# Earlier loads and a new order of small steps in a hybrid attention kernel: mask and two weights loaded a stage sooner, first output blocks split inside the last gates, new tokens' steps that end a slot, a later turn of mixer B's factors

## The chip, the core and the metric

The program runs on one core of one Trainium2 chip. A core has five engines that each work through a queue of their own, in order: TensorE (PE; its weight loads are shown apart as PEld) multiplies matrices, VectorE (DVE), ScalarE (ACT) and GpSimd (POOL) work on elements, and SyncE (SP) only issues transfers here. Sixteen DMA engines move data. The metric is the device time of one execution in microseconds (us), lower is better, given as the median of several runs.

## The reference, cut to what matters

One layer of a decoder: a prompt of 2048 tokens and 8 new tokens, width 1024.

```python
def _prompt_layer(x, w_in, sinks, w_o, ln_g, ln_b):
    qa, ka, va, ga, qb, kb, vb, gb = _project(x, pos, w_in)      # rotary on the first quarter of each head
    parts = []
    for _, d in ((128, 1), (512, 4), (2048, 16)):                # mixer A: 8 heads, three strided bands
        m, den, o = _band_partial(_dilate(qa[:, :, :, None], d), _dilate(ka, d), _dilate(va, d))
        parts.append((_undilate(m, b, s, d), _undilate(den, b, s, d), _undilate(o, b, s, d)))
    oa = _merge(parts)
    m, den, o = _band_partial(qbg, kb, vb)                       # mixer B: 8 heads, band of 128, sinks
    ob = _merge([(m, den, o)], sink)
    mix = concat([oa * silu(ga), ob * silu(gb)])
    return layer_norm(ALPHA * x + mix @ w_o)
```

`_merge` weighs partial outputs by exp(m - max) and divides by the summed denominators; the factor of each row and pattern is what the text calls **the factors**. The new tokens do the same against a cache. All results are float32; the large products are made from a high and a low part (h and l) of each operand, three matmuls for one.

## The kernel before, in words

**Stages.** First (0 to about 242 us) the projections of K and Q. Then the values' stage (242 to 378 us): V for all tokens in two column groups, and between its matmuls the new tokens' attention of mixer A, whose cached values (`vc`, six loads of 1 MB) feed the `soa` matmuls of line 444. Then the attention stage (378 to about 980 us), then the output projection with the layer norm.

**The attention stage** is written out by hand inside `tc.manual_schedule` (line 1117): each engine gets the instructions of this region in the order in which the program emits them. Instructions outside the region are ordered by a planner on a simulated clock; it may put them between the region's instructions but cannot change the order of those. The main loop runs over 66 **groups** i. A group makes the scores of one quarter of a job (a job is one pair of heads at one dilation: 12 for mixer A, 4 for mixer B), turns (transposes) the weights of group i-1 and multiplies the values of group i-2. It has four **slots** (sl = 0 to 3). In each slot `advance(870 ns)` draws matmuls from `follow`, which is a stream of other PE work: first the projections of mixer B's queries and of the gates in three passes (line 628, 24 matmuls for one block, each worth n / 2.4 ns), then the first blocks of the output projection (line 671, each worth 213 ns). A `yield None` in `follow` ends the slot's share. Then `step()` runs `tick()` (pending small jobs; one or two quarters of a raw weight are split on GpSimd) and moves the first of the **chains** on by one step.

**Chains** wait their turn: only the first of the list moves. `merge_b` (line 945), one for each of mixer B's four pairs, computes the factors on DVE and ACT (952 to 960), turns them on PE (line 965), writes them to memory (970), fetches them spread over 64 partitions on GpSimd's queue (982) and multiplies the outputs (992), the last pair's on DVE alone. A step between two `yield`s takes one slot. Its turn waits for slot 3 (`while where[0] < 3`).

**Raw weights.** `Parts` (line 113) puts four quarters of a weight in a queue; `raw_step` loads two quarters in a tick into one of four small buffers and splits a quarter on GpSimd three ticks later. The weights of QB2 and G0, third and fourth of the first pass, come in this way from the stage's first tick on; those of QB0 and QB1 are split before.

**The mask** `mk` (128 x 768) is loaded after the values' stage (line 563) and negated (line 1121) ahead of the first `weights` (line 832), whose `mk` operand is its 128 columns from 128 on in the first job.

**PSUM.** Gate blocks (`pg`), the new tokens' small products of mixer B (`scb`, `spt`, `sob`, `spo`, made by `sample("b")` one step after each gate block of the last pass) and the first output blocks share two banks (tag `mm`). A gate block frees its bank when ACT (line 167) and, one tick later, DVE (line 171) have read it.

**The first output blocks.** At the start of the last gate block row `gated(0)` loads gate and mixed output of tokens 0 to 255. `out_weights` (line 720) asks for the last two output weights (four empty slots), splits that block (739, 740), and then runs 12 matmuls for each half of token blocks 0 and 1, loads and splits the next 256 tokens after that, with three more empty slots, and goes on with token blocks 2 and 3. What the loop hasn't drawn when it ends is emitted outside the region (lines 1162 to 1164).

Of the kernel before, what the change touches and what calls it, by code (L numbers as in the profile page):

```python
# [11 lines left out]
F32 = mybir.dt.float32  # L12
# [38 lines left out]
def hymba_step(ctx, tc, xt, xs, xr, wq, wv, wo, tab, msk, ident, diag, sinks, lng, lnb,  # L51
# [61 lines left out]
    class Parts:  # L113


        def __init__(self, src, hl=None):
            self.hl, self.left = hl, 4
            raws.extend([self, src, k0, None, 0] for k0 in range(0, 8, 2))
# [9 lines left out]
    def raw_step(now=False):  # L128

        for r in raws:  # L130
            r[4] += r[3] is not None
        for _ in range(2):
            if raws and raws[0][0].hl and raws[0][3] is not None and (now or raws[0][4] >= 3):
                p, _, k0, w, _ = raws.popleft()
                h, l = p.hl
                G.tensor_copy(h[:, k0:k0 + 2], w)
                G.tensor_sub(l[:, k0:k0 + 2], w, h[:, k0:k0 + 2].bitcast(F32))
                p.left -= 1
        for r in [r for r in islice(raws, RAW) if r[3] is None][:2]:
            r[3] = at.tile([128, 2, 128], F32, name="raw", bufs=RAW)  # L140
            dma(r[3], r[1][:, r[2]:r[2] + 2])
# [197 lines left out]

    def sample(nm, sp, sk):  # L340
# [29 lines left out]
        if A:  # L370
            z = z.rearrange("p n i c -> p n (i c)")
        else:
            snc = sp.tile([128, 1], F32, name="snc")
            dma(snc, dram(sinks, 0, [[0, 16], [1, 8], [1, 1]]))
            kcs = []
            for t in range(2):
                kc = sk.tile([128, 4, w], F32, name="kc", tag="cache", bufs=2)
                dma(kc[:, :, :w - 1], kcb[:, 4 * t:4 * t + 4])
                kcs.append(kc)
            yield  # L380
            yield
            for t, kc in enumerate(kcs):
                V.tensor_copy(kc[:, :, w - 1], kself[:, 0, 4 * t:4 * t + 4])
            yield
        p = ps.tile([128, 512], F32, name="sc" + nm, tag="mm")
# [29 lines left out]
        yield  # L415
        pt = ps.tile([128, 512], F32, name="spt", tag="mm")
# [16 lines left out]
        for t in range(2):  # L433
            if A or t == 0:
                oa = ps.tile([128, 512], F32, name="so" + nm, tag="mm")
# [33 lines left out]
        yield  # L469
        pt = ps.tile([128, 512], F32, name="spo", tag="mm")  # L470
# [7 lines left out]
    first = {}  # L478

    def load_first():  # L480

        for n, src, h0 in (("k", ks, 2), ("q", qa, 0)):
            t = first[n] = kp.tile([128, SEQ], F32, name=n)
            for h in range(2):
                dma(t[64 * h:64 * h + 64], src[:, h0 + h, :SEQ])
        v = first["v"] = kp.tile([128, 16, 128], F32, name="v")
        dma(v, vs[1].rearrange("(p r) c -> p r c", r=16))
# [77 lines left out]
    def stream(passes):  # L565

        with tc.tile_pool(name="gw", bufs=1, side="right", reuse_waits="tile") as gw, \
# [31 lines left out]
            for i in (2, 3):  # L599
                ws[passes[0][i]] = Parts(wq[TILES.index(passes[0][i])])  # L600
                weights(i, passes[0][i])
            for pi, names in enumerate(passes):
# [7 lines left out]
                for c, c2 in zip(route, route[1:] + [None]):  # L610
# [3 lines left out]
                    if c2 is None:  # L614
                        for name in more:
                            ws[name] = Parts(wq[TILES.index(name)])
                        if not more:
                            head.append(gated(0))
                            wo_parts.update((i, Parts(wo[:, i].rearrange("p (a b) -> p a b", b=128))) for i in (4, 5))
                    for i, name in enumerate(names):  # L620
# [12 lines left out]
                        if news:  # L633
                            next(news, None)
                        if c2 is None:
                            if not more and i < 2:
                                soon(lambda i=i: first_wo(i), 1)
                            for e in range(i, len(more) if name == names[-1] else min(i + 1, len(more))):
                                soon(lambda e=e, name=more[e]: weights(e, name), 1)
# [4 lines left out]
    queries, wo_parts = [], {}  # L644
# [59 lines left out]
    head = []  # L704
# [15 lines left out]
    def out_weights():  # L720
# [6 lines left out]
        nxt = head[0]  # L727
        first.clear()
        for j in range(2):
            t, g = nxt  # L730
# [4 lines left out]
            for _ in range(1 if j == 0 else 2):  # L735
                yield None
            h, l = [oh.tile([128, 4, 256], F32R, name="h" + a) if j else kept.tile([128, 4, 256], F32R, name="h" + a, tag="p%d" % (i + 2))
                    for i, a in enumerate("hl")]
            V.tensor_mul(t, t, g)
            split(h, l, t, V)  # L740
            yield None
            if j == 0:
                nxt = gated(1)
            for tb, x in zip((2 * j, 2 * j + 1), xs_):
# [6 lines left out]
                first[tb] = x, 4  # L751

# [3 lines left out]
    class Job:  # L756
# [69 lines left out]
        def weights(self, g, us):  # L826
            for u in us:
# [4 lines left out]
                V.tensor_tensor_reduce(sm[:, :w], self.s[:, h, n % 4, :w], mk[:, MI[self.d], 256 - w:], -0.125, 3.0e38,  # L832
# [112 lines left out]
    def merge_b(job):  # L945
# [16 lines left out]
        while where[0] < 3:  # L962
            yield
# [153 lines left out]
    with tc.manual_schedule(engines=set(ENGINES)):  # L1117
# [3 lines left out]
        V.tensor_scalar(mk, mk, -1.0, None, op0=OP.mult)  # L1121
        jobs[0].fetch_q(0)
        for i in range(N + 2):
# [19 lines left out]
            for sl in range(4):  # L1143
# [6 lines left out]
                where[0] = sl  # L1150
                advance(RATE / 4 if i else RATE / 2)
# [10 lines left out]
    ascope.close()  # L1162
    for _ in follow:
        pass
# [176 lines left out]
```

## Time and profile before

| | |
|---|---|
| median of 3 runs | 1188.15 us (1187.61 to 1189.95) |
| profiled execution, its own time | 1187.53 us |
| its span, first to last instruction | 1185.7 us |
| mean granted TensorE clock | 0.987 |
| PE, PEld, DVE, ACT, POOL busy | 95, 85, 46, 37, 35 % of the span |
| DMA | 230.14 MB, mean 194 GB/s |

A span lies inside the time of its execution, 1.8 us shorter here. Matmul ends are modelled, so PE busy does not mean PE at its peak. Idle time of an engine counts only where the end hangs on it. Three things are read together: the waits of PE (who let it go on, and after how long), the granted clock in short stretches, and the timeline of the other engines at the same moment. In a timeline row stand start, duration, engine, line, operation, output<-inputs, count, and in brackets the idle time before it and what ended it.

### The profile page before, as it was taken

The numbers are of one execution on the slowest core, as the hardware profiler recorded it, in microseconds if no ns is written. First come the engines' busy times: TensorE is split into PE (matmuls) and PEld (weight loads), VectorE is DVE, ScalarE is ACT, GpSimd is POOL, SyncE is SP. The second block draws the span as 40 slices with busy tenths as digits, with TensorE's granted clock in tenths as the row PEclk, the third lists the DMA queues.
The fourth block names the chain that finished last, engine by engine and source line by source line (L and its number), as shares of the span: only waits on it lengthen the run. The fifth ranks groups of instructions, "written<-read, shape, count | busy, mean of one in ns | idle before, by whom it ended". The sixth has DMA issues, their size and how long they took to land.

```text
span 1185.7 us, 23404 instructions
## 1 busy us (share of the span) xinstructions
PE 1131.9 (95%) x8614; PEld 1002.3 (85%) x8614; DVE 547.6 (46%) x1784; ACT 437.9 (37%) x1416; POOL 416.2 (35%) x559
## 2 busy tenths in 40 slices
PE   7999999999999899999999999999998988999995
PEld 7899999997978788898888789888887866688884
DVE  6532000101002465465566556666657664775543
ACT  4300011111101566556656555555554541232221
POOL 2243010310001300046715603670574454476541
PEclk9999999999999999999999999999999998999998
DMA  8854988366396664489688868968989667556521
GB/s 277 257 146 144 272 272 280 108 195 203 124 325 200 188 163 141 136 193 202 172 235 185 197 211 193 195 159 239 229 184 276 183 189 231 169 153 199 186 87 69
DMA packets 194002, 230.14 MB, mean 194 GB/s; under 512 B 34608, under 2 KB 160208, under 8 KB 193504
## 3 DMA queue, kind: packets, MB, share of 16 engines
q1 hardware_dynamic: 188640, 211.87, 59.3%
q0 software_dynamic: 5248, 16.78, 9.2%
q8 instruction: 67, 1.10, 0.4%
q14 instruction: 47, 0.39, 0.1%
HBM read 158.52 MB, written 70.07 MB: 193 GB/s over the span
## 4 chain that ended last, share of the span: by engine, by line
PE 69%; DMA 13%; POOL 4%; DVE 4%; ACT 3%; issue 3%; SPq 1%; DVEq 0%; POOLq 0%; ACTq 0%
PE po L671 14%; PE pg L628 13%; PE pv L526 7%; PE ps_s L824 7%; PE ps_o L875 6%; DMA F<-fd 6%; PE ps_pt L854 5%; PE ps L151 4%; PE pmm L151 4%; PE ppt L151 4%; PE po L151 3%; ACT pe L835 2%; DMA wvf<-in_wv 1%; POOL F L1054 1%; POOL oT L1055 1%
## 5 line engine op out<-in xcount | busy, mean ns | idle before, releaser
L835 ACT ACTIVATE pe<-sm,st 128x256 f32<-128x256 f32 (+1 forms) x512 | 236.6, 464 | 206.2 <-DVE st L832 204.8
L832 DVE CUSTOM_DVE_ANT_0 sm<-ps_s,mk 128x256 f32<-128x256 f32 (+1 forms) x512 | 180.2, 375 | 182.8 <-PE ps_s L824 116.2
L628 PE MATMUL pg<-gx,gw 128*128 128x256 f32 (+1 forms) x1104 | 166.7, 294 | 4.4 <-DVE mixS L476 2.1
L628 PEld LDWEIGHTS pg<-gx,gw 128*128 128x128 f32 x1104 | 142.5, 192 | 5.1 <-issue 4.3
L854 PE MATMUL ps_pt<-idt,pe 128*128 128x128 f32 x848 | 135.2, 280 | 5.7 <-ACT oT L892 2.8
L860 DVE COPY pT<-ps_pt 128x512 f32<-128x512 f32 x176 | 120.6, 685 | 6.8 <-PE ps_pt L854 6.6
L1040 POOL DMA_DIRECT2D F<-fd x64 | 41.2, 647 | 209.7 <-DMA fd<-wts 202.9
L854 PEld LDWEIGHTS ps_pt<-idt,pe 128*128 128x128 f32 x848 | 96.4, 142 | 19.6 <-issue 8.7
L875 PE MATMUL ps_o<-pT,v 128*64 128x128 f32 (+1 forms) x1120 | 106.8, 335 | 0.0
L875 PEld LDWEIGHTS ps_o<-pT,v 128*64 128x64 f32 x1120 | 70.1, 137 | 39.5 <-issue 16.5
L835 ACT ACTIVATION_READ_ACCUMULATOR pe<-sm,st 128x1 f32 x512 | 96.3, 188 | 0.0
L824 PE MATMUL ps_s<-k,qo 64*128 64x256 f32 (+1 forms) x768 | 91.8, 379 | 0.0
L628 PE MATMUL pg<-gx,gw2h 128*128 128x256 f32 (+1 forms) x368 | 75.6, 294 | 2.1 <-ACT spe L405 2.1
L824 PEld LDWEIGHTS ps_s<-k,qo 64*128 64x128 f32 x768 | 66.7, 188 | 12.4 <-issue 1.3
L526 PE MATMUL pv<-wvh,xh 128*128 128x384 f32 (+1 forms) x224 | 69.6, 311 | 0.0
L526 PE MATMUL pv<-wvh,xl 128*128 128x384 f32 (+1 forms) x224 | 69.5, 310 | 0.0
L526 PE MATMUL pv<-wvl,xh 128*128 128x384 f32 (+1 forms) x224 | 69.4, 310 | 0.0
L628 PEld LDWEIGHTS pg<-gx,gw2h 128*128 128x128 f32 x368 | 58.7, 192 | 2.4 <-ACT spe L405 2.4
L671 PE MATMUL po<-wl,mho 128*128 128x512 f32 x192 | 59.7, 392 | 0.0
L538 ACT ACTIVATE vf<-pv 128x384 f32<-128x384 f32 (+1 forms) x32 | 14.0, 437 | 111.8 <-PE pv L526 61.6
L628 PE MATMUL pg<-gx,gw2l 128*128 128x256 f32 (+1 forms) x184 | 54.2, 294 | 0.0
L259 POOL TENSOR_TENSOR wl<-w,wh 128x512 fp32r<-128x512 f32 x18 | 24.2, 1356 | 82.8 <-DVE wh L258 82.8
(260 smaller groups left out, 2521.0 us busy)
## 6 DMA issues: line engine op xcount, KB each, us to landing
gx<-xd SPq DMA_DIRECT2D x80, 512.0 KB
F<-fd POOLq DMA_DIRECT2D x80, 192.0 KB, 7.1
gs<-th SPq DMA_DIRECT2D x64, 128.0 KB
v<-vs SPq DMA_DIRECT2D x28, 256.0 KB
xd<-xh SPq DMA_DIRECT2D x12, 512.0 KB
xd<-xl SPq DMA_DIRECT2D x12, 512.0 KB
kc<-in_kca SPq DMA_DIRECT2D x8, 768.0 KB
vc<-in_vca SPq DMA_DIRECT2D x6, 1024.0 KB
```

The source lines that it names most:

```text
L151: T.matmul(p[:, :n], a[:, kt, :], b, start=k == 0, stop=k == 23)
L259: (V if between else G).tensor_sub(l[:, k0:k0 + 4], w, h[:, k0:k0 + 4].bitcast(F32))
L526: T.matmul(p[:, :w], l, r[:, kt, :w], start=k == 0, stop=k == 23)
L628: T.matmul(p[:, :n], a[:, kt, :], b[:, kt % 2, :n], start=kt + e == 0, stop=kt == 7 and e == 2)
L671: T.matmul(p, a, b[:, nh * 4:nh * 4 + 4].rearrange("p a b -> p (a b)"), start=first and k == 0, stop=last and k == end)
L824: T.matmul(s[:, h, n % 4, :w], self.Q[g][r, n % 4 * 128:n % 4 * 128 + 128], self.keys(n)[r], start=True, stop=True)
L832: V.tensor_tensor_reduce(sm[:, :w], self.s[:, h, n % 4, :w], mk[:, MI[self.d], 256 - w:], -0.125, 3.0e38, op0=OP.add, op1=OP.min, accum_out=m)
L835: S.activation(p[:, :w], sm[:, :w], AF.Exp, scale=-1.0, bias=m, accum_out=den)
L854: T.transpose(pt[:, h, j], self.P[h, n][:, a:a + 128], idt)
L860: V.tensor_copy(t, pt)
L875: T.matmul(o[64 * h:64 * h + 64, a:a + 128 * len(ns)], v[:, cv, kv:kv + 64], t[:, h, j:j + len(ns)].rearrange("p a b -> p (a b)"), start=n ...
L1040: G.dma_start(F[a * 64:a * 64 + 64], dram(fd, a * 3 * SEQ + c * 256, [[0, 64], [SEQ, 3], [1, 256]]))
```

## The change

Four edits. **Loads:** `load_first`, in the values' stage, also loads the first job's 128 mask columns (64 KB) and the raw weights of QB2 and G0 (two loads of 512 KB), ahead of the first K, Q and V; they take a buffer of the K and of the Q tiles. The quarters of these two weights are then split in the first four ticks with no load of their own. The whole mask is negated three slots into group 1. **First output blocks:** `first_split`, seven ticks after the last gate block row begins, splits tokens 0 to 255; the next 256 are split right after token block 0's products; four of the empty slots are gone, and what is left of `follow` is emitted inside the region. **New tokens:** after each of their four steps that makes a product in PSUM, `follow` yields 1200 ns, which ends the slot and takes from the next. **Factors:** for the first three of mixer B's pairs two more `yield`s stand ahead of the turn.

```diff
-        def __init__(self, src, hl=None):
+        def __init__(self, src, hl=None, here=None):
             self.hl, self.left = hl, 4
-            raws.extend([self, src, k0, None, 0] for k0 in range(0, 8, 2))
+            raws.extend([self, src, k0, None if here is None else here[:, k0:k0 + 2], 3] for k0 in range(0, 8, 2))
...
         for r in raws:
-            r[4] += r[3] is not None
+            r[4] = r[4] + 1 if r[3] is not None else 0
...
     def load_first():
+        early_w = kp.tile([128, 2, 8, 128], F32, name="raw01", tag="k", bufs=2)
+        early_m = kp.tile([128, 128], F32, name="mk1", tag="q", bufs=2)
+        dma(early_m, msk[:, 0, 128:256])
+        for i in range(2):
+            dma(early_w[:, i], wq[TILES.index(FIRST[2 + i])])
+        first["m"], first["w"] = early_m, early_w
...
-                ws[passes[0][i]] = Parts(wq[TILES.index(passes[0][i])])
+                ws[passes[0][i]] = Parts(wq[TILES.index(passes[0][i])], None, first["w"][:, i - 2])
...
                         if not more:
                             head.append(gated(0))
+                            early_split.append(soon(first_split, 7))
...
                         if news:
+                            parting.clear()
                             next(news, None)
+                            if parting:
+                                yield 1200
...
+    def first_split():
+        t, g = head.pop()
+        h, l = [kept.tile([128, 4, 256], F32R, name="h" + a, tag="p%d" % (i + 2)) for i, a in enumerate("hl")]
+        V.tensor_mul(t, t, g)
+        split(h, l, t, V)
+        halves.append((h, l))
+        head.append(gated(1))
...
+        here = blocks(0)
+        yield None
+        for j in range(2):
+            h, l = halves[j]
+            for tb, x in zip((2 * j, 2 * j + 1), here):
...
                 first[tb] = x, 4
+                if tb == 0:
+                    here = blocks(1)
+                    t, g = head.pop()
+                    h2, l2 = [oh.tile([128, 4, 256], F32R, name="h" + a) for a in "hl"]
+                    V.tensor_mul(t, t, g)
+                    split(h2, l2, t, V)
+                    halves.append((h2, l2))
...
-                V.tensor_tensor_reduce(sm[:, :w], self.s[:, h, n % 4, :w], mk[:, MI[self.d], 256 - w:], -0.125, 3.0e38,
+                V.tensor_tensor_reduce(sm[:, :w], self.s[:, h, n % 4, :w], (mk[:, MI[self.d], 256 - w:] if self is not jobs[0] else first["m"]), -0.125, 3.0e38,
...
         while where[0] < 3:
             yield
+        if job.of.pair < 3:
+            yield
+            yield
         pst = ps.tile([128, 512], F32, name="pst", tag="pt", bufs=2)
...
-        V.tensor_scalar(mk, mk, -1.0, None, op0=OP.mult)
+        V.tensor_scalar(first["m"], first["m"], -1.0, None, op0=OP.mult)
...
+                if i == 1 and sl == 3:
+                    V.tensor_scalar(mk, mk, -1.0, None, op0=OP.mult)
...
-    ascope.close()
-    for _ in follow:
-        pass
+        ascope.close()
+        for _ in follow:
+            pass
```

`parting` gets an entry in `sample` ahead of each of the four PSUM tiles; `blocks(j)` loads the two input blocks that `for tb, x` uses, as the removed lines did.

More of the change, by code (lines that the diff above doesn't have):

```diff
@@ L338, in hymba_step @@
                     EMIT[TILES[i][0]](pw, NC, p, TILES[i], c0, n)
+    parting = []
     def sample(nm, sp, sk):
@@ L384, in sample @@
             yield
+        parting.append(0)
         p = ps.tile([128, 512], F32, name="sc" + nm, tag="mm")
@@ L415, in sample @@
         yield
+        parting.append(1)
         pt = ps.tile([128, 512], F32, name="spt", tag="mm")
@@ L434, in sample @@
             if A or t == 0:
+                parting.append(2)
                 oa = ps.tile([128, 512], F32, name="so" + nm, tag="mm")
@@ L469, in sample @@
         yield
+        parting.append(3)
         pt = ps.tile([128, 512], F32, name="spo", tag="mm")
@@ L642, in stream @@
                 pass
-    queries, wo_parts = [], {}
+    queries, wo_parts, early_split = [], {}, []
     ready, merged, resident = [], [], []
@@ L702, in norm @@
         dma(y[tb * 128:tb * 128 + R], x[:R])
-    head = []
+    head, halves = [], []
+    def first_split():
[5 more added lines that the diff above has]
+        head.append(gated(1))
     def gated(j):
@@ L726, in out_weights, with blocks @@
         oh = wscope.enter_context(tc.tile_pool(name="oh", bufs=1, side="right", reuse_waits="tile"))
-        nxt = head[0]
         first.clear()
-        for j in range(2):
-            t, g = nxt
+        if not halves:
+            early_split[0].run()
+        def blocks(j):
             xs_ = [(oh if tb < 3 else kp).tile([128, D], F32, name="xh%d" % tb, **(dict(tag="k", bufs=2) if tb == 3 else {}))
@@ L734, in out_weights @@
                 dma(x, xr[tb * 128:tb * 128 + 128])
[L735 to L744, printed above, removed]
+            return xs_
+        here = blocks(0)
[3 more added lines that the diff above has]
+            for tb, x in zip((2 * j, 2 * j + 1), here):
                 cols = slice(tb % 2 * 128, tb % 2 * 128 + 128)
```

## The prediction

> **What bounds the kernel now.** First the page: PE is the bound in total, so the question is where it waits and where its clock falls. Columns: busy us, share of the span, instructions.
>
> ```profile
> span 1185.7 us, 23404 instructions
> PE 1131.9 (95%) x8614; PEld 1002.3 (85%) x8614; DVE 547.6 (46%) x1784; ACT 437.9 (37%) x1416; POOL 416.2 (35%) x559
> ```
>
> Second the waits of PE between 300 and 1020 us: who let it go on, us in total, times, longest.
>
> ```profile
> PE pg L628 <- ACT qf L181: 4.7, 1, 4.7
> PE pst L965 <- DVE wts L960: 4.7, 2, 2.4
> PE po L671 <- DVE xh L750: 3.4, 1, 3.4
> ...
> PE po L671 <- ACT hh L108: 2.6, 2, 2.3
> PE pg L628 <- ACT spe L405: 2.1, 1, 2.1
> PE pg L628 <- DVE mixS L476: 2.1, 1, 2.1
> PE pg L628 <- issue: 1.7, 1, 1.7
> PE po L671 <- DVE hl L109: 1.0, 2, 0.5
> ```
>
> Each edit answers one of these: the loads the first, the factors the second, the output blocks the third, fourth and last, the new tokens the three between. Third, short stretches. Columns: us, busy us (instructions) of PE, PEld, DVE, ACT, POOL, granted clock, DMA share, GB/s.
>
> ```profile
> 390.20:393.60 3.40, 3.40 (x18) 3.18 (x17) 0.00 (x0) 0.00 (x0) 2.12 (x5) 0.51 0.65 200
> 840.70:844.10 3.40, 1.28 (x22) 0.87 (x22) 2.33 (x8) 3.22 (x14) 2.95 (x5) 0.99 0.92 221
> 844.10:847.50 3.40, 3.40 (x16) 3.40 (x17) 2.82 (x8) 0.73 (x3) 3.31 (x6) 0.50 0.88 169
> 878.30:881.70 3.40, 3.40 (x18) 3.40 (x18) 2.53 (x5) 0.60 (x2) 2.95 (x6) 0.51 0.41 42
> 960.20:963.60 3.40, 3.40 (x18) 1.93 (x16) 1.53 (x8) 1.09 (x4) 0.00 (x0) 0.51 0.39 102
> 980.70:984.10 3.40, 3.40 (x9) 2.67 (x10) 2.24 (x7) 0.26 (x1) 1.88 (x4) 0.51 0.99 275
> 1001.20:1004.60 3.40, 3.40 (x10) 2.67 (x9) 0.81 (x2) 0.00 (x0) 1.50 (x3) 0.52 0.90 236
> 927.90:931.30 3.40, 3.40 (x35) 2.52 (x36) 1.81 (x10) 0.88 (x4) 0.00 (x0) 1.00 1.01 319
> ```
>
> A stall is often followed by 3.4 us at half clock (0.50 to 0.52), which loses 1.7 us more: six such stretches stand here. The starts lie on one grid of some 3.4 us (960.2, 980.7 and 1001.2 are 20.5 apart, six steps). Not every stall pays: behind the one of 2.3 us that ends at 927.73 the clock stayed at 1.00 (last row).
>
> [...]
>
> **The change, part by part.** The sum is against the profiled execution, 1187.5 us (span 1185.7 and 1.8 around it); the median of the runs shown is 0.6 higher.
>
> *Loads.* Timeline (start, duration, engine, line, operation, output<-inputs, count, [idle before <-releaser]) and two longer stretches:
>
> ```profile
> 379.14 6.09 PE L628 MATMUL pg<-x,gw 128*128 128x264 f32 x48
> 385.22 0.56 DVE L1121 TENSOR_SCALAR mk<-mk 128x768 f32<-128x768 f32 x1 [8.32 <-DMA mk<-in_msk]
> 385.70 0.40 POOL L136 CAST gw2h<-raw 128x256 fp32r<-128x256 f32 x1 [14.06 <-DMA raw<-in_wq]
> 389.93 0.64 PE L628 MATMUL pg<-x,gw2h 128*128 128x264 f32 x2 [4.70 <-ACT qf L181]
> 323.50:358.00 34.50, 31.90 (x268) 27.55 (x266) 2.26 (x4) 2.69 (x7) 1.43 (x2) 1.00 1.05 332
> 358.00:378.00 20.00, 19.53 (x180) 17.61 (x176) 6.03 (x18) 3.45 (x9) 4.47 (x6) 1.00 0.50 146
> ```
>
> The mask lands at 385.2, after 8.3 us in which DVE has nothing to do, the raw weight not before 385.7; the DVE and ACT work of group 0 queues behind the negation, and the `pg` bank that PE wants comes free only behind that, at 389.9. With both resident the first negation runs at once, POOL splits four ticks early, and eight raw loads leave SP's queue there. The second negation (0.56 us, three slots into group 1) lies under PE's gate matmuls; uncovered it would cost 0.56. So -4.7, and -1.7 for the half-clock stretch at 390.2. The price: 64 KB and two times 512 KB, 1.11 MB, join the values' stage. At 332 GB/s, where the engines were full (share 1.05), they take 3.4 us; the 20 us after that have a share of 0.50. I take a third, 1.1, since most queue positions fall where there is slack; bounds 0 and 5.1 (all of it on PE, and one half-clock stretch). Net -5.3, bounds -6.4 to -1.3.
>
> *New tokens.* Their small steps wait for ACT or DVE work that the same slot queued before. Turns and gates in a slot:
>
> ```profile
> 856.41 0.60 PE L854 MATMUL ps_pt<-idt,pe 128*128 128x128 f32 x4
> 856.76 1.19 PE L628 MATMUL pg<-gx,gw 128*128 128x256 f32 x8
> ...
> L860 DVE COPY pT<-ps_pt 128x512 f32<-128x512 f32 x176 | 120.6, 685 | 6.8 <-PE ps_pt L854 6.6
> ```
>
> A slot that ends there lets PE go on with the job's turns; two fill 0.35 to 0.4 us each (856.41 to 856.76), so each of the three waits (2.1, 1.7, 2.1) shrinks by 0.8: -2.4. I count one half-clock stretch as avoided, -1.7. Against that, four slots lose their gate matmuls, and the copies of their turns (0.69 us) are covered only by the next turns (0.35): four slots, two copies, 0.34 each, +2.7. The put-off work itself, 4 x 1200 / 106.7 = 45 matmuls (5.7 us at 6.09 / 48), is not lost but ends the gates five to six slots later. Net -1.4; bounds -9.3 (5.9 of waits and two stretches gone) and +2.7 (only the copies).
>
> *Factors.* Rows of pair 1's turn and what follows:
>
> ```profile
> 927.73 0.27 PE L965 MATMUL pst<-idt,wts 128*32 128x128 f32 x1 [2.29 <-DVE wts L960]
> 932.33 2.09 POOL L982 DMA_DIRECT2D F<-fd  x4 [4.80 <-DMA fd<-stT]
> 937.06 1.81 POOL L992 TENSOR_TENSOR oT<-oT,F 128x768 f32<-128x768 f32 x1 [2.64 <-DMA F<-fd]
> ```
>
> Two steps are two slots, far above the 2.3 us by which `wts` is late. So -4.7, and -1.7 for the stretch at 960.2. The turn now falls in slot 1 instead of 3, between the job's turns, with the same two banks: a copy of 0.69 may delay each of three: 0 to +2.1, I take +1.0. Net -5.4, bounds -6.4 to -4.3. The price is elsewhere: only the first of the chains moves, so each pair passes two slots (and what it waits for slot 3) to the next. Counting the `yield`s, turns of pairs 0 to 2 go from slot 3 of groups 56, 59, 62 to slot 1 of 57, 61, 65, and pair 3's from group 65 to nine steps behind the loop.
>
> *The tail.* From the last value matmuls to the new tokens' block. DVE rows, the group of multiplications, its landing times, and the chain that ended last:
>
> ```profile
> 975.06 1.95 PE L875 MATMUL ps_o<-pT,v 128*64 128x256 f32 x20
> 980.38 0.38 DVE L952 SCALAR_TENSOR_TENSOR mn<-snk,st 128x32 f32<-128x32 f32 x1
> 983.21 0.19 DVE L960 SCALAR_TENSOR_TENSOR wts<-wts,dn 128x32 f32<-128x32 f32 x1
> 984.70 0.69 DVE L750 SCALAR_TENSOR_TENSOR xh<-xh,po 128x512 f32<-128x512 f32 x1 [1.29 <-PE po L671]
> 990.97 1.22 DVE L739 TENSOR_TENSOR ht<-ht,hg 128x1024 f32<-128x1024 f32 x1
> 993.31 1.23 DVE L109 TENSOR_TENSOR hl<-ht,hh 128x1024 fp32r<-128x1024 f32 x1 [1.13 <-ACT hh L108]
> L992 DVE TENSOR_TENSOR oT<-oT,F x6: 692/952/1059, 914.1 to 1006.0; 128x768 f32<-128x768 f32 x5, 128x512 f32<-128x512 f32 x1
> DMA to landing us min/median/max: 2.8/4.3/10.0
> 1010.81 7.00 PE po L161 x64
> 1017.81 146.93 PE po L671 x634
> ```
>
> Before: 977.0 to 1010.8, 33.8 us, with 96 first-block matmuls (22.3 us at 146.93 / 634 = 0.232), two half-clock stretches and the waits. After, block 0 is split inside the gates, so PE starts at once; but DVE keeps the written order, in which pair 2's multiplication stands ahead of the sum of the first block (L750), of the split of block 1 and of pair 3's factors. From pair 2's turn, near the end of the values: to `F`'s issue 4.6 (927.73 to 932.33), landing 4.7 (to 937.06), POOL's part 1.8, DVE's 0.95, L750 0.7, split 3.6 (990.97 to 994.54), factors 3.0 (980.38 to 983.40): 19.4 to pair 3's turn. PE has a third of the 96 matmuls ahead of it (32 or 33, 7.7 us) and stands for about 11.7. From that turn 4.6 + 4.7 + 0.95 + 1.0 (a second issue) + 4.7 + two multiplications of 0.7, and 2.8 for the last output block (12 matmuls), 20.1; queued behind each are L750s, hence `po`'s two banks. Together 39.5, and two half-clock stretches as now, 3.4: 42.9. The planner may put part of the 7.0 us of the new tokens' block (L161, outside the region) into the gap; I take 2.5 (bounds 0 and 7.0): 40.4, which is +6.6 (bounds +2.1 and +9.1, above that the first rival). The splits on POOL of the last two weights come some steps later, under the same gap.
>
> Sum: -5.3 - 1.4 - 5.4 + 6.6 = -5.5, so **1182.0 us**.
>
> **The rivals.**
>
> *The chain in the tail sets the end* (slower). Nothing is pulled into the gap (+2.5) and one `F` of pair 3 lands after 10.0 us, the longest row above, instead of 4.3 (+5.7): 1182.0 + 8.2 = 1190.2. It decides when the tail exceeds 33.8 + 12.1 (the three gains) = 45.9. For it: two of these loads stand in a row, and DMA shares of 0.90 to 0.99 in the stretches there. Against: the median of 4.3.
>
> *PE stays fed.* The tail has more than I see that doesn't hang on DVE, and the waits of today (3.4 + 2.6 + 1.0 = 7.0) and two half-clock stretches (3.4) go: -12.1 - 10.4 = 1165.0. For it: block 0's products start under the last values. Against: the DVE order.
>
> *The early loads only move the wait, and the tail is no worse or better.* -6.4 + 3.4 + 1.7 = -1.3; the edits in the gates give nothing, because a slot that ends meets the next unready chain: about 1186.0, within what can be told. For it: share 1.05 in the values' stage.
>
> **How the numbers follow.** Forecast 0.40 (own range 1177.5 to 1186, from the whole block pulled in, 4.5 below, to loads and new tokens half way to their upper bounds, 4.0 above), slower rival 0.25, fed PE 0.10, no change 0.25. A measurement of this kernel can tell some 0.2%, 2.4 us (the runs shown span 1187.61 to 1189.95). Of the last, 0.03 falls below that bound and 0.02 above; of the slower rival 0.03 falls within it. Faster 0.40 + 0.10 + 0.03 = 0.53, same 0.20 + 0.03 = 0.23, slower 0.22 + 0.02 = 0.24. The range reaches 10 down towards the fed PE, of which it leaves out most, and up to 1194, where a second landing is late by two thirds of 5.7: 1172 to 1194 leaves out about 0.07 below and 0.10 above.
>
> **What would show it.** Loads: PE's wait at 385 gone and POOL's `gw2h` cast before 380 us; right if values still end near 378.05, wrong if later by 2 or more. New tokens: waits of `pg` between 840 and 912 about 3.5 instead of 6. Factors: no wait of `pst` within the gates. Tail: a new wait `pst` <- `wts` of 8 to 12 us behind the last values, then `po` <- `xh`; the L161 block before or after the last `po`; three of the six half-clock stretches gone (390, 960 and one of 844 and 878). Wrong: a tail under 30 us (the fed PE), or over 46 (slower).

## The result and the profile after

The changed kernel takes 1197.66 us (median of 5 runs, 1196.86 to 1205.08) against 1187.61 (5 runs) for the kernel before: ratio 1.0097, 95% interval 1.0068 to 1.0127, some 11.5 us slower (the medians differ by 10.1). The forecast was 1182.0 and faster. The profiled execution took 1199.82 us.

First the page of the changed kernel, and four long pieces of the chain that ended last (start, us, what). Line numbers are those of the changed kernel: 628 became 642, 671 became 688, 750 became 774, 860 became 891, 965 became 999, 982 became 1016, 992 became 1026.

```profile
span 1197.8 us, 23412 instructions
PE 1133.0 (95%) x8614; PEld 1002.5 (84%) x8614; DVE 544.6 (45%) x1785; ACT 438.2 (37%) x1416; POOL 416.2 (35%) x559
```

```profile
986.26 8.99 DMA F<-fd
1008.39 4.75 DMA mgo<-gs
1022.86 7.00 PE po L161 x64
1029.86 146.94 PE po L688 x634
```

PE does the same work (8614 matmuls, 1133.0 us against 1131.9) in a span 12.1 us longer. The new tokens' block (L161) starts 12.05 us later, at 1022.86 against 1010.81, and from there on both kernels are alike. So all is lost before it. The first two pieces, a load of pair 2's factors and one of gates for a later output block, come up again below. Now the waits of PE between 300 and 1040 us (us in total, times, longest):

```profile
PE po L688 <- DVE xh L774: 10.4, 3, 7.4
PE ps_pt L885 <- DVE pT L891: 8.3, 11, 2.5
PE pst L999 <- DVE wts L991: 6.8, 1, 6.8
...
PE spo L477 <- DVE od L473: 2.8, 1, 2.8
PE pg L642 <- ACT th L424: 1.7, 1, 1.7
PE pg L642 <- DVE mixS L482: 1.5, 1, 1.5
...
PE ps_s L855 <- ACT vf L551: 1.2, 1, 1.2
PE pg L642 <- ACT spe L408: 0.8, 1, 0.8
```

The copies' waits in the kernel before, for comparison:

```profile
PE ps_pt L854 <- DVE pT L860: 2.4, 6, 1.1
```

The waits that the edits were aimed at are gone or smaller: `qf` 4.7 (gone), `pst` within the gates 4.7 (gone), the new tokens' 2.1, 1.7 and 2.1 (now 1.7, 1.5 and 0.8). But others stand in their place: 2.8 and 1.2 at the end of the values' stage, copies (`pT`) 8.3 instead of 2.4, and behind the loop 10.4 + 6.8 instead of 3.4 + 2.6 + 1.0.

By stage, from the timeline of PE (us; "tail" is from the end of the last value matmuls to the new tokens' block):

| | before | changed | changed, second profile |
|---|---|---|---|
| first scores (the values' stage ends) | 378.05 | 384.27 | 381.07 |
| first scores of group 2 | 393.57 | 394.85 | 392.31 |
| last values end | 977.0 | 977.1 | 973.4 |
| tail | 33.7 | 45.7 | 44.9 |

Of the three gains of 12.1 us that the forecast had ahead of the tail nothing is left at the end of the values in the first profile and 3.6 us in the second, and the tail is 11 to 12 us longer. The chain of the tail, in a timeline of the changed kernel (start, us, engine, line, operation, [idle before <-releaser]):

```profile
978.57 0.27 PE L999 MATMUL pst<-idt,wts 128*32 128x128 f32 x1
978.69 1.84 SPq L141 DMA_DIRECT2D raw<-in_wo  x4
983.62 1.48 SPq L141 DMA_DIRECT2D raw<-in_wo  x2
985.15 0.90 SPq L761 DMA_DIRECT2D xh<-in_xr  x2
984.68 2.10 POOL L1016 DMA_DIRECT2D F<-fd  x4
991.11 0.69 DVE L774 SCALAR_TENSOR_TENSOR xh<-xh,po 128x512 f32<-128x512 f32 x1 [11.32 <-DMA xh<-in_xr]
991.86 1.22 PE L688 MATMUL po<-wl,hh 128*128 128x512 f32 x2 [7.44 <-DVE xh L774]
995.37 0.96 DVE L1026 TENSOR_TENSOR oT<-oT,F 128x768 f32<-128x768 f32 x1 [3.57 <-DMA F<-fd]
996.85 1.62 DVE L780 TENSOR_TENSOR ht<-ht,hg 128x1024 f32<-128x1024 f32 x1
999.59 1.22 DVE L109 TENSOR_TENSOR hl<-ht,hh 128x1024 fp32r<-128x1024 f32 x1 [1.12 <-ACT hh L108]
1002.49 0.19 DVE L991 SCALAR_TENSOR_TENSOR wts<-wts,dn 128x32 f32<-128x32 f32 x1
1002.83 0.37 PE L999 MATMUL pst<-idt,wts 128*32 128x128 f32 x1 [6.77 <-DVE wts L991]
```

PE starts block 0 at once (978.6), and stops after two halves: the sums wait for `xh`, whose loads stand behind six raw loads in SyncE's queue. Then VectorE waits for pair 2's `F` (995.37), issued on GpSimd at 984.68, and behind that multiplication stand the second sum, the second split and pair 3's factors. PE has nothing for 7.4 and 6.8 us. The granted clock adds to it (columns as before: us, busy of the engines, clock, DMA share, GB/s):

```profile
920.90:924.30 3.40, 2.84 (x14) 2.62 (x14) 2.66 (x8) 1.46 (x4) 3.18 (x6) 0.50 0.17 47
934.50:937.90 3.40, 3.40 (x16) 3.09 (x18) 1.50 (x5) 1.58 (x4) 0.00 (x0) 0.51 0.62 218
...
985.50:988.90 3.40, 0.00 (x0) 0.00 (x0) 0.00 (x0) 0.00 (x0) 3.23 (x7) 1.00 0.83 260
989.00:992.40 3.40, 0.55 (x1) 0.50 (x2) 0.69 (x1) 0.00 (x0) 2.90 (x6) 0.53 1.01 262
992.40:995.80 3.40, 3.40 (x9) 2.31 (x7) 0.43 (x1) 0.00 (x0) 1.50 (x2) 0.50 1.03 311
...
999.20:1002.60 3.40, 0.00 (x0) 0.00 (x0) 2.46 (x8) 0.62 (x2) 1.35 (x3) 0.53 0.47 144
1002.60:1006.00 3.40, 3.17 (x9) 2.52 (x10) 1.05 (x3) 0.00 (x0) 1.91 (x3) 0.50 0.11 16
```

In and behind each of the two long gaps lie two stretches at half clock, not one.

### The profile page after: what moved, and what is told of

Read it like the earlier page. It is cut to its first block, busy times and chain, and to the rows that moved or that the text cites. A ratio compares the mean times of both kernels' runs of the same rounds, so it can differ in the third digit from the quotient of the medians.

```text
span 1197.8 us, 23412 instructions
## 1 busy us (share of the span) xinstructions
PE 1133.0 (95%) x8614; PEld 1002.5 (84%) x8614; DVE 544.6 (45%) x1785; ACT 438.2 (37%) x1416; POOL 416.2 (35%) x559
## 4 chain that ended last, share of the span: by engine, by line
PE 66%; DMA 17%; POOL 5%; issue 3%; ACT 3%; DVE 3%; SPq 2%; DVEq 0%; POOLq 0%; ACTq 0%
PE po L688 13%; PE pg L642 12%; DMA F<-fd 7%; PE ps_s L855 6%; PE pv L539 6%; PE ps_o L906 6%; PE ps_pt L885 5%; PE ps L151 5%; PE pmm L151 5%; PE ppt L151 5%; PE po L151 3%; ACT pe L866 2%; DMA wvf<-in_wv 1%; POOL F L1088 1%; POOL oT L1089 1%
```

## The experiments

The later runs scatter more than the first (kernel before: 1178.6 to 1200.0 over all of them), so ratios against the kernel before on the same chip are compared, with their intervals. Waits and tails come from one profile each; two kernels with the tail of before unedited had 33.6 and 35.6, so a tail is good to some 2 us.

**The changed kernel again** (no edit).

> The changed kernel once more, nothing edited. Its profile has two waits of PE for the cached keys (kc, 1.1 and 1.8 us) and a half-clock stretch at 279 us which the kernel before doesn't show, 3.8 us in all, at a point where the instructions of both kernels still stand in the same order. If that is the scatter of the transfers, the values' stage ends here some 2.5 us later than before (378.05) instead of 6.2, and the median stays at 1197.7 or a little below. If it belongs to the changed kernel, 6.2 again.

1.0075 [1.0049, 1.0100]. Values' stage ends at 381.07, 3.0 later than before: the waits for cached keys and the half-clock stretch at 279 in the first profile were scatter.

**Factors undone.**

```diff
-        if job.of.pair < 3:
-            yield
-            yield
```

> The changed kernel without the two further yields ahead of the turns of pairs 0 to 2; the other three edits stay. Theory (the chain in the tail): each pair hands two slots to the next, so without them pair 3's turn lies in the loop again, the wait of 6.8 us for pair 3's wts and one half-clock stretch of 3.4 us that loses 1.7 are gone, the two waits of pst at about 2.3 come back and the copies' waits of 2.5 and 2.0 go: 1197.7 - 8.5 = about 1189. Rival (the tail is set by the late loads of xh and by the work of PE left for it, whatever the pairs do): 1195 or more.

1.0036 [1.0012, 1.0060]: 4.6 us better than the changed kernel on the same chip, half of what the theory had. Pair 3's turn comes 6 us behind the last values (979.5) instead of 26, its wait is 4.8 instead of 6.8, but the tail is still 43.5: PE waits 10.0 us for sums. Neither the theory nor the rival alone.

**xh loaded first.**

```diff
+        oh = wscope.enter_context(tc.tile_pool(name="oh", bufs=1, side="right", reuse_waits="tile"))
         wO = wscope.enter_context(tc.tile_pool(name="wO", bufs=1, side="right", reuse_waits="tile"))
...
+        here = blocks(0)
         for kt in (6, 7):
...
-        oh = wscope.enter_context(tc.tile_pool(name="oh", bufs=1, side="right", reuse_waits="tile"))
...
-        here = blocks(0)
         yield None
```

> The changed kernel with the two loads of xh (tokens 0 to 255, 1 MB) issued ahead of the raw loads of the last two output weights instead of behind them; only SyncE's order changes. Theory (two causes in a row): the 7.4 us that PE waits at 984.4 for xh go, but the next thing in PE's order, pair 3's turn, waits for DVE, which waits for pair 2's F at 995.4 whatever xh does; PE comes to it earlier and stands there longer, so 1 to 3 us are gained: about 1195.5. Rival (the late xh alone costs 7.4 and its half-clock stretches): about 1187.

1.0094 [1.0063, 1.0126]: no gain at all. Waits of PE behind the loop:

```profile
PE pst L999 <- DVE wts L991: 16.0, 1, 16.0
PE po L688 <- DVE xh L774: 1.9, 1, 1.9
```

7.4 and 6.8 became one wait of 16.0, tail 45.4. The late `xh` was on the page as the longest wait and worth nothing: the next piece in PE's order hung on the same VectorE queue.

**Loads alone on the kernel before** (its part of the change's diff).

> The kernel before with the loads' edit alone (mask columns and two raw weights in the values' stage, splits without loads, late negation of the whole mask). The prediction's step: -5.3, about 1182.3. Reading of the two profiles (the stage ends 2.5 later because the cached values come later, and the wait of 4.7 and one half-clock stretch are saved behind it): about -2.5, 1185. Rival (the wait only moves): within 1 of before, 1187.

0.9970 [0.9947, 0.9993]: some 3.6 us faster, by its interval 0.8 to 6.3. In its profile (waits of PE; two stretches):

```profile
PE spo L471 <- DMA vs<-vf: 2.8, 1, 2.8
PE ps_s L830 <- ACT vf L544: 1.5, 1, 1.5
```

```profile
380.30:383.70 3.40, 1.89 (x15) 1.70 (x17) 0.49 (x4) 0.77 (x2) 2.75 (x5) 0.54 0.91 249
383.70:387.10 3.40, 3.40 (x20) 3.18 (x16) 1.02 (x8) 0.50 (x2) 0.00 (x0) 0.50 1.03 338
```

The wait of 4.7 is gone, but the stage ends at 382.06 instead of 378.05, and group 2 starts at 393.50 instead of 393.57. In this pair of profiles the wait has only moved. All profiles kept say the same: in the nine with the loads' edit (the run below with later raw loads left out) the values' stage ends at 382.3 on the mean and group 2 starts at 393.4, in the ten without it at 378.8 and 393.6. So the stage ends 3.6 us later and the start of group 2 is where it was. The times say that on the mean a little is left; where that little comes from isn't shown.

**New tokens alone; factors alone; output blocks alone**, each on the kernel before, with its part of the change's diff.

> The kernel before with the 1200 ns yields alone. The prediction's step: -1.4, 1187. Reading of the profiles (the waits of pg at the new tokens' steps fall from 6.5 to 4.2 us, a wait of 1.3 for a copy comes, one half-clock stretch as before; 45 matmuls, 5.7 us, go to the tail, where PE waits anyway): -1 to -2. Rival (the gates end 1.5 us behind the last values, so the first output blocks and with them the whole tail come later): +2 to +5.

1.0037 [1.0011, 1.0062], tail 41.1: the rival's time, slower by 4.4 us; its reason falls below. The waits at their steps fell as read, the tail took more back.

> The kernel before with the two further yields alone. The prediction's step without the tail: -5.4, about 1183. Theory (the wait for pst only turns into waits for the copies behind the factors and multiplications on VectorE, and the pairs' chain runs into the tail, where VectorE's order puts the multiplications ahead of the sums that free po's banks): no gain in the loop, +4 to +8 behind it: about 1194.

1.0015 [0.9991, 1.0040], tail 37.4: between the two. In the loop the pairs' waits did go here, and copies' waits of 1.5 and 1.5 came; behind it PE waits 4.9 for pair 3's factors.

> The kernel before with the output blocks' edit alone (first split inside the gates, second behind token block 0's products, four empty slots fewer, the rest inside the region). By the prediction PE starts at once and the waits of 2.6 and 1.0 for hh and hl go: -3, about 1185. Theory (the sums of the first block wait for xh, which now stands behind the raw weights in SyncE's queue, and the second split stands behind pair 3's multiplications): a wait of some 7 us comes for them, +3 to +5, about 1192.

1.0031 [1.0006, 1.0056], tail 36.2, with a wait of 6.7 for pair 3's factors, which now stand behind the first sum, and that behind `xh`. As the theory had it, by 3.7 us. The four alone add up to +0.53%, some 6.3 us of the 9 to 11.5. Each of the four intervals reaches some 3 us to both sides, so the times can't show whether the rest is what the edits do to each other; one such effect, in the copies' waits, is shown further down.

**Raw weights loaded later.**

```diff
     def load_first():
-        for i in range(2):
-            dma(early_w[:, i], wq[TILES.index(FIRST[2 + i])])
...
                     S.activation(vf[:, :w], p[:, :w], AF.Copy)
+                    if nt == 27:
+                        for i in range(2):
+                            S.activation(first["w"][:, i, 0, :1], vf[:, :1], AF.Copy)
+                            dma(first["w"][:, i], wq[TILES.index(FIRST[2 + i])])
```

> The loads' edit alone, but the two raw weights are loaded behind the sixth load of cached values instead of ahead of the third (a ScalarE copy of one column into their buffer, from a value block three later, holds them back). Theory (in the other place the 1 MB pushes the cached values back, the new tokens' last step slips behind the last value block and PE waits 2.8 + 1.5 us there): with the cached values as early as before, most of the 4.3 us at the stage's end and one half-clock stretch go: 4 below the loads alone, -5 to -6 against before. Rival (the transfers are full anyway and the wait stays): no better than the loads alone, -2.

1.0004 [0.9977, 1.0031]: no better than in the other place. The waits at the stage's end fell to 0.7 and 0.6, but 3.4 for cached values and 2.9 for `qf` stand in its profile. The theory fell; where the price of the loads sits stays open.

**New tokens, nothing taken from the next slot.**

```diff
                             if parting:
-                                yield 1200
+                                yield None
```

> The new tokens' edit alone, but the slot is ended by a yield of None, which drops only what is left of the slot (at most 870 ns, on the mean some 435) and takes nothing from the next: some 16 gate matmuls are put off instead of 45. Theory (the put-off gates cost the 7 us that the tail of the new tokens' edit alone is longer, 41.1 against 33.7): the last gate ends ahead of the last values again, the tail is 34 to 37, the time -1 to +1 against before. Rival (the four slots without gates cost it, not what is put off): +4 as with 1200.

1.0041 [1.0019, 1.0063]. The gates end ahead of the last values (965.3 and 969.4) and the tail is 41.0 all the same, with these waits: 

```profile
PE po L680 <- DVE xh L759: 8.3, 1, 8.3
PE po L680 <- ACT hh L108: 3.9, 1, 3.9
```

So it isn't the amount put off. VectorE's rows ahead of the longer wait:

```profile
993.85 0.83 DVE L668 TENSOR_TENSOR mto<-mto,mgo 128x256 f32<-128x256 f32 x2 [4.79 <-DMA mgo<-gs]
994.60 0.95 DVE L1001 TENSOR_TENSOR oT<-oT,F 128x768 f32<-128x768 f32 x1
995.47 0.68 DVE L759 SCALAR_TENSOR_TENSOR xh<-xh,po 128x512 f32<-128x512 f32 x1
```

The sum that frees PE (995.47) stands behind pair 3's first multiplication, and that doesn't wait for its `F` here but stands behind `mto`, the gating of mixed outputs for the output projection (`mixed`, outside the hand-ordered region, put there by the planner), for whose gates `mgo` VectorE waits 4.79. In the kernel before the same place stands in the chain that ended last, and its sum costs PE 3.4:

```profile
993.89 4.29 DMA mto<-ms
```

Written as letters, VectorE's order from pair 3's factors (W) on is, with S the sum of an output block's half, H the second split, M a multiplication of pair 3: before W S S S H M S M S M S, with `yield None` W S S H M S M M S S: one sum fewer ahead of H, of `mto` and of the first M.

**Another later turn.**

```diff
-        while where[0] < 3:
+        while job.of.pair == 0 and where[0] < 3:
             yield
+        yield
```

> The kernel before with another way to a later turn: one further step ahead of every pair's turn, and only pair 0 waits for slot 3. Counted in steps, the turns of pairs 0 to 2 come one, two and three steps later than before and pair 3's four, instead of two, six, ten and some ten more. Theory (the gain of the factors' edit lies in the loop, some 4 us, its price in the steps handed on to pair 3): most of the gain at a quarter of the price, tail 34 to 35, -3 against before. Rival (the waits only turn into waits for the copies): 0 to +2.

1.0025 [1.0003, 1.0046], some 3.0 us slower, tail 38.3: nearer to the rival, but not for its reason. The waits for `pst` are gone and the copies' are only 1.4 us longer than before (3.8 against 2.4); the price lies behind the loop, where four steps later for pair 3 cost as much as ten (37.4).

**xh first, and pair 2's second multiplication on GpSimd.**

```diff
-            (V if c == 1 or kt == 7 else G).tensor_mul(o[:, cc], o[:, cc], Fs[c])
+            (V if kt == 7 or (c == 1 and kt < 6) else G).tensor_mul(o[:, cc], o[:, cc], Fs[c])
```

> The changed kernel with xh loaded first (as in the run before) and, for pair 2, the second multiplication on GpSimd instead of VectorE, so that VectorE doesn't wait for pair 2's F ahead of the second split and pair 3's factors. Theory (this order sets the tail, wait of 16.0 us for pair 3's wts with xh first): the wait falls to 8 to 11, the tail from 45.4 to about 39, 5 to 6 faster than the changed kernel: about +3 against before. Rival (pair 3's factors are late for the steps alone): the wait stays at 14 or more, +9.

1.0071 [1.0043, 1.0099], tail 45.6. Pair 3's factors did come earlier, and a sum then waited for its multiplications instead:

```profile
PE po L688 <- DVE xh L774: 11.3, 1, 11.3
PE pst L999 <- DVE wts L991: 4.5, 1, 4.5
```

16.0 + 1.9 became 4.5 + 11.3. Taking one piece out moves the wait to the next, so neither theory nor rival: no single piece sets the tail.

**The changed kernel without the 1200 ns.**

```diff
                             next(news, None)
-                            if parting:
-                                yield 1200
```

> The changed kernel without the 1200 ns yields; the other three edits stay. If the edits' costs add up: 4.5 off, about +4.5 against before, the last gate ahead of the last values and the tail near 40. If the tail is set by the chain of pair 3 alone, whenever the gates end: no gain, +8 to +9, tail 44 to 46.

1.0022 [1.0001, 1.0044]: by the middle values more came off than the edit costs alone, but the intervals overlap. The tail is 30.4 in its profile, though pair 3's turn still waits 5.8 us there; behind the new tokens' block a wait of 3.4 for `mlo` on GpSimd and a half-clock stretch give 5.1 back, so that from the end of the values it is 2 us longer than before (198.4 against 196.6 to the last matmul). Without the yields the gates end 13 us ahead of the last values (958.9 and 972.3), and more of the output blocks lies in front of the chain. From the end of the values to the last matmul the changed kernel takes 208.5 us, so the yields cost it 10 us there, against the 7 that they cost alone: a difference little above the scatter of a tail.

**More of the output blocks in each step behind the loop**, on four kernels.

```diff
         while chains or fetches:
-            advance(RATE / 4)
+            advance(RATE / 2)
```

> The changed kernel with xh loaded first and with 1740 ns instead of 870 of follow's matmuls drawn in each step behind the loop, so that more sums of output blocks stand ahead of the pairs' factors and multiplications in VectorE's order. Theory (the order of these small pieces sets the tail: two of eight sums ahead of pair 3's factors with xh first, four now): PE's waits behind the loop fall from 18 to about 10, the tail from 45.4 to 37-38: about +2 against before. Rival (pair 3's chain of transfers sets the end, in whatever order the sums stand): tail 44 or more, +9.

1.0009 [0.9980, 1.0037], tail 37.9, as expected. PE's only wait behind the loop:

```profile
PE po L688 <- DVE xh L774: 10.7, 2, 9.6
```

Nothing but the number of matmuls drawn per step differs from the run with the wait of 16.0; the transfers and their number are the same. So the order in which the small pieces meet cost about 7.5 us of the tail of the kernel with xh first, and by the times (1.0094 against 1.0009, intervals apart) some 10. What is left of the wait stands again behind `mto`: the chain has 6.30 us for a load of `mgo` there (993.83).

> The kernel before with 1740 ns drawn in each step behind the loop. Theory: four sums instead of three stand ahead of the second split and pair 3's first multiplication, but the second split now stands behind all four, so PE waits for it; -1 to +1, tail 33 to 35. Rival (every step that draws less than PE can do costs time): tail 30, -3.

1.0030 [1.0001, 1.0059], tail 36.0: worse than expected: PE waits 8.8 for `hh`, the second split now stands behind all four sums.

> The new tokens' edit alone with 1740 ns drawn in each step behind the loop. It tells what makes its tail 7 us longer, though the yield that puts off only a third of the matmuls had the same tail (41.0). Theory (the output blocks start one to two steps later against pair 3's chain, so two sums instead of three stand ahead of its multiplications): drawing more sets them in order only partly, since the first two sums still stand ahead of the multiplication alone: tail 38 to 41. Rival (what is put off has to be drawn again): tail 34, the time that of before.

1.0067 [1.0035, 1.0100], tail 44.4: not better than without (1.0037, the intervals overlap), and the tail is beyond the theory's 38 to 41 too. The rival (what is put off has to be drawn again) falls.

> The factors' edit alone with 1740 ns drawn in each step behind the loop. In VectorE's order four sums and the second split now stand ahead of pair 3's factors, and three more sums ahead of its multiplications. Theory (order in the tail): the price behind the loop (37.4 against 33.7) goes, the gain in the loop stays: tail 33 or less, -3 to -5 against before, which would be faster than both kernels. Rival (pair 3's transfers, four more steps late, set the end): tail 37 to 40, +2.

1.0015 [0.9986, 1.0043]. The tail did fall to 32.4, but the time isn't better than the factors alone. In its profile the loop from group 2 on is 7.8 us longer than in that of the factors alone, 5.1 of it longer waits for `oT`, 2.2 of these for that of mixer A's last merge (below); what the factors gain in the loop isn't seen in the times.

**New tokens with the step restored, and with the loads.** The share of a slot is raised from 870 to 875 ns (`RATE` 3480 to 3500) beside `yield None`. VectorE's order in its profile is W S S H S S M M S S M S: four sums ahead of the first M instead of two, but still two ahead of H (the third stands inside the second split). With the loads' edit too it is W S S S H S M M S S M S, three ahead of H as before.

> The new tokens' edit alone with a yield of None, and a share of 875 ns in each slot instead of 870, so that the put-off matmuls are drawn again over the whole loop and the output blocks start at the same step against pair 3's chain as before: in VectorE's order three sums stand ahead of the second split and pair 3's multiplications again. Theory (this order made the tail 7 us longer): tail 33 to 35 instead of 41.0, the shorter waits in the loop (4 us) stay: -2 to -4 against before, faster than both kernels. Rival (the tail is longer for another reason): tail 40, +4.

0.9984 [0.9959, 1.0009], against 1.0041 without the raised share. Waits of PE between 400 and 1012 us:

```profile
PE po L680 <- ACT hh L108: 5.0, 1, 5.0
PE po L680 <- DVE xh L759: 4.6, 1, 4.6
PE pst L974 <- DVE wts L969: 3.7, 3, 2.5
```

No wait of a new tokens' step is left, and the tail is 37.3: half of the 7 us came back, not all.

> The same together with the loads' edit. The loads alone gave 0.997 of before. If the two add up: -4 to -6 against before, tail 33 to 35; if the loads only move a wait, the same as without them.

0.9969 [0.9945, 0.9992], 2.7 us below before by medians: faster than both kernels, and no better than the loads alone (0.9970). The tail is 37.7, though three sums stand ahead of H again: what makes it longer than 33.7 stays open.

## Why the prediction was wrong

The two profiled executions lie 12.3 us apart where -5.5 was forecast, a miss of 17.8. Some 12.2 of it are the three gains, of which nothing has arrived at the end of the values, and 5.4 are the tail. In the second profile it is 8.5 and 4.6. So the larger part failed ahead of the tail.

**Loads** (-5.3, bounds -6.4 to -1.3). Right in direction by the times: alone 0.8 to 6.3 us faster. The price of 1.1 was too low in the profiles: the stage ended 3.0 (second profile) and 4.0 (loads alone) later, 3.6 on the mean of all profiles, in the upper half of the bound of 5.1, and the half-clock stretch at 390 wasn't saved but came at 380, twice as long. "Most queue positions fall where there is slack" was the weak step: both raw loads went out ahead of the third and fourth load of cached values, and the new tokens' last product, ahead of the last value block before, came behind it. By its own sign (wrong if the values end later by 2 or more) the step fell; of 5.3 us, 0.2 are left at the start of group 2, and the third rival was right in this: the wait moved.

**New tokens** (-1.4). The waits fell from 6.5 (0.5 of them for `th`) to 4.0, 2.5, as the sum had it (2.4). The step that failed is "not lost but ends the gates five to six slots later", which was priced at nothing: alone it cost 7 us in the tail. The runs put the cause in the step at which the output blocks start against pair 3's chain (a third of the amount had the same tail; moving the sums forward again brought back the time, and half of the tail). The other half isn't explained.

**Factors** (-5.4). The wait of `pst` was to go, and "a copy of 0.69 may delay each" was to cost 1.0, at most 2.1. In the changed kernel the copies cost more. DVE, and PE's waits for it:

```profile
919.52 1.28 DVE L1026 TENSOR_TENSOR oT<-oT,F 128x768 f32<-128x768 f32 x1 [1.49 <-DMA F<-fd]
920.73 0.68 DVE L891 COPY pT<-ps_pt 128x512 f32<-128x512 f32 x1
921.46 1.12 PE L885 MATMUL ps_pt<-idt,pe 128*128 128x128 f32 x4 [2.48 <-DVE pT L891]
932.99 0.72 DVE L991 SCALAR_TENSOR_TENSOR wts<-wts,dn 128x32 f32<-128x32 f32 x1
933.63 0.68 DVE L891 COPY pT<-ps_pt 128x512 f32<-128x512 f32 x1
934.36 0.97 PE L885 MATMUL ps_pt<-idt,pe 128*128 128x128 f32 x4 [2.02 <-DVE pT L891]
965.94 0.66 PE L885 MATMUL ps_pt<-idt,pe 128*128 128x128 f32 x4 [0.99 <-DVE pT L891]
```

The factors still take VectorE's time, and at 933.6 the job's copy stands behind them instead of the turn; at 919.5 pair 0's multiplication, which waits for its `F`, holds a copy too. With a third of 1.0 that is 5.5 us, more than the 4.7 saved, and half-clock stretches stay (934.5 above, and 920.9). What was overlooked: the wait wasn't for the turn alone but for VectorE, and everything else that VectorE makes for PE waits in the same queue. And the term of 1.0 fails only where two edits meet. With the factors and without the 1200 ns the copies' waits are 3.3 to 4.1 us in three profiles, at most 1.7 more than before, within the bound; with the 1200 ns and without the factors 2.1 to 2.7, in three; with both 7.4 to 10.8, in five. In all five VectorE stands 1.5 to 5.1 us for pair 0's `F` ahead of such a copy, and in the three with the factors and without the 1200 ns it doesn't stand there. (With the 1200 ns alone it stands there too, 1.5 to 5.1, but PE doesn't wait for it; why stays open.) So adding up the gains of the edits as if they were independent was a false step of the sum. The chain's price in steps was seen, and right in kind.

**The tail** (+6.6, bounds +2.1 to +9.1; measured +12.0 and +11.2). The mechanism was the one forecast: pair 2's multiplication ahead of the sum, the split and pair 3's factors, PE standing in front of pair 3's turn. From that turn to the end it took 20.0 us (1002.83 to 1022.86), with 20.1 forecast. The equal length is luck in its pieces: GpSimd issued pair 3's `F` 2.5 us after the turn (1005.37) instead of 4.6, and VectorE's first multiplication came 8.1 after that (1013.51) instead of 4.7, behind two `mto` that waited for `mgo` (4.75 in the chain above). Up to the turn 25.7 (977.1 to 1002.83) stood against 19.4, 1.5 of it ahead of pair 2's turn. The mis-sized term is `F`: issue 6.1 us after pair 2's turn instead of 4.6 (978.57 to 984.68), and 10.7 from there to VectorE's multiplication (995.37), against 4.7 and 1.8 of GpSimd's part. A landing like the slowest one, which the slower rival used for pair 3 with 10.0, came for pair 2 (8.99 in the chain). And the planner put nothing of the new tokens' block into the gap (2.5), though 14 us were free. The late loads of `xh`, noted nowhere in the sum, gave the longest wait of the page and cost nothing of their own. The `mto` pieces have no term in the sum either; their loads stand in the chain of the kernel before too (4.29), and no run takes them out, so what they cost isn't shown.

**The rivals.** The slower one came nearest, and in part by luck. The tail of 45.7 lay just under the 45.9 from which it was to decide, and under its own 48.6 (40.4 and 8.2); yet the kernel was slower than its 1190.2, because it kept the three gains of 12.1, of which the two profiles show between nothing and 3.6 us at the end of the values. The range ended at 1194 for the same reason: no case let both sides fail together, though both hang on VectorE's queue.

**The clock.** Behind PE's waits of 2.48 and 2.02 us the granted clock was 0.50 and 0.51 for 3.4 us (the stretches at 920.9 and 934.5 above); in and behind the gaps of 7.4 and 6.8 us it was 0.53 and then 0.50 for two such stretches each (989.0 to 995.8, 999.2 to 1006.0). The length of a wait alone doesn't tell it: behind the 2.29 us that end at 927.73 in the kernel before the clock stayed at 1.00.

## What to carry to other kernels

When an edit takes away a wait for an in-order engine, list everything else that the same engine does for the waiting one, in written order; the wait goes to the next item unless the work itself goes. A piece of work put off by a few slots may cost nothing where it runs, but it can change its place against other chains further on: compare the order of the small pieces where the two streams meet, before and after. Gains of edits that work through the same engine don't simply add up: the copies' waits grew by at most 1.7 us with one edit and by 5.0 to 8.4 with two. And a long wait on the page is worth only the distance to the next wait behind it: of 7.4 us for `xh`, none.

## What was not expected of the hardware

- In and behind the gaps of 7.4 and 6.8 us the clock was granted at half for 6.8 us (two stretches of 3.4 us each, 0.53 and 0.50), while PE stood through part of them; behind the waits of 2.48 and 2.02 us it was 3.4 (0.50 and 0.51).
- The wait of PE for mixer A's last merge (`oT`, near 680 us), where all these kernels have much the same work, was between 1.1 and 6.6 us from profile to profile. A single profile can't show a change of 3 us in the loop.
